# Input projection of a decoder trunk: 512 moving columns for the matmuls, halves added on eviction, the key norm moved, the convolution's taps regrouped

## The chip, the cores and the metric

One core of a Trainium2 chip runs the kernel. The metric is the device time of one execution in microseconds (us); the kernel before was run three times, with a median of 1014.74 us (1014.39 to 1015.14).

## What is computed

One decoder layer on a sequence of 256 tokens with 2048 channels, in float32. The input is normalised, projected once, and the columns of the projection are divided among three token mixers:

```python
x = layer_norm(x, ln_in_g, ln_in_b)
h = jnp.einsum("bsd,dc->bsc", x, w_in[l])                 # 2048 -> 2368 columns
c_q, c_kv, k_rope = h[..., :o1], h[..., o1:o2], h[..., o2:o3]
u_conv, u_pool = h[..., o3:o4], h[..., o4:]
y_mla  = mla_mixer(c_q, c_kv, k_rope, ...)                # 8 heads, latent q (512) and kv (256), rotary key
y_conv = conformer_conv_mixer(u_conv, ...)                # a*sigmoid(g), causal convolution of 31 taps, LN, silu
y_pool = pool_mixer(u_pool, ...)                          # trailing mean over 2/4/8/16 minus token, linear
x = layer_norm(ALPHA * x + concat(y_mla, y_conv, y_pool) @ w_out[l], ln1_g, ln1_b)
# then w_up, a convolution of 3 taps, silu gate, w_down, and a third layer norm
```

## The kernel before, in words

Channels lie on partitions, tokens along the free side, so one activation tile is 128 x 256. Every large product is made of three: weights and activations are each split into a rounded high part and the rest (`hi`, `lo` for weights; `xh`, `xl`, called x in the profile, for activations), and high*high, high*low and low*high are added in one PSUM bank. For each channel tile kt the normalised input holds `xh` and `xl` beside each other, so that both can be read as one operand of 512 columns (`X.wide(kt)`).

Weights come in units of 128 x 2048 from HBM (SP's DMA queue, two pieces of 128 x 1024). For each piece ACT rounds `hi<-raw` (line 198) and DVE subtracts `lo<-raw,hi` (line 214). `take()` hands the next unit to TensorE and stages a later one, so these two operations stand in the instruction streams several units ahead of their use.

The input projection takes its units in this order: four pairs for the convolution (value and gate of 128 channels each), a pair for the latent kv (`kvb`), one unit for the rotary key (`kr`, line 614), two pairs for the latent q, two pairs for the pooling mixer. The first convolution pair is done while the input is normalised. All other pairs go through `proj`: for each of 16 channel tiles and 2 column blocks three matmuls of 256 columns, 48 for a unit. The FFN and the kr unit already use 512 moving columns, in `proj_wide` and a loop of its own.

Between the matmuls the program puts DVE work on a queue `bgq`: for each of the four convolution tiles `acc` a first tap (`tap0`, line 573) and 30 more (line 576, `acc<-hp,pc,acc`). `bg(n)` takes n of them out, behind every unit; the table NBG holds n for convolution units, kv, kr and q units, pooling units, ukv and uq units, and units of w_out. What is left is taken out before the convolution's layer norm.

Behind the projection follow, on TensorE: the keys of 8 heads (KN, from `ckh`, `ckl`), the values V, two units of the queries (QR with the rotary part, QN), the rotations (`rope`, a matmul, and three DVE operations a tile, lines 627 to 629), the pooling mixer's linear map (line 759), and the scores of the first two heads. These read KN and QN in a first matmul and the rotated key KA and the rotated query qn[0] in a second, which must wait until DVE has finished `rope` of the first tile.

The pooling mixer (`pool_group`) copies a projected tile to `up` (ACT, line 682), forms the trailing sums on POOL by doubling (`ws`, line 687: one, two, three, four additions for the four windows), and subtracts on DVE (`dd`, line 690). Each engine runs its instructions in the order of the program.

Of the kernel before, what the change touches and what calls it, by code (L numbers as in the profile page):

```python
# [12 lines left out]
AF = mybir.ActivationFunctionType  # L13
ALU = mybir.AluOpType

P = 128
S = 256
NTB = S // P
D = 2048
KT = D // P  # L20
# [6 lines left out]
NCONV = 31  # L27
# [8 lines left out]
LASTG = 3 + NTAIL  # L36
BY_PE = 2
WARM0 = 44
NBG = (4, 4, 4, 4, 4)
RES_AT = (4, 5, 8, 11)  # L40


# [40 lines left out]
def build(tc, ctx, a, out):  # L83
    nc = tc.nc
    act, dve, pool, pe, sp = nc.scalar, nc.vector, nc.gpsimd, nc.tensor, nc.sync
    sub, mul, add = ALU.subtract, ALU.mult, ALU.add
# [54 lines left out]
    def PC(name, i=0):  # L141
        return pc[:, _PC[name] + i:_PC[name] + i + 1]

    ident = C("ident", 0, 128)
# [89 lines left out]
    def take():  # L234
        while len(staged) < LOOK + 1 and nxt[0] < len(units):
            stage_one(homes[nxt[0] - len(units)] if nxt[0] >= len(units) - NTAIL else None)
        return staged.popleft()
# [3 lines left out]
    def bg(n):  # L241
        while n > 0 and bgq:
            bgq.popleft()()
            n -= 1
# [10 lines left out]
    def mm(o, l, r, start, stop):  # L255
        pe.matmul(o, l, r, start=start, stop=stop)  # L256
# [86 lines left out]
    def m(name="m", dt=F32, w=S):  # L343
        return mp.tile([P, 288], dt, tag="m", name=nm(name), bufs=28)[:, 0:w]
# [4 lines left out]
    def pbg(n):  # L349
        while n > 0 and pq:  # L350
            pq.popleft()()
            n -= 1
# [88 lines left out]
    X = Channels("x")  # L441
# [65 lines left out]
    xh, xl = [X.hi(k) for k in range(KT)], [X.lo(k) for k in range(KT)]  # L507
# [3 lines left out]
    res_in = residual_ops(dve, a["ln_in_g"], a["ln_in_b"])  # L511


    def proj(nun, kper, ncb, ah, al, banks, nbg=0, total=None):
        total = total or nun * kper
        for u in range(nun):
            w = take()
            for k in range(kper):
                kt = u * kper + k
                s0, s1 = kt == 0, kt == total - 1  # L520
                for cb in range(ncb):
                    c = (k * ncb + cb) * P
                    o = banks[cb][:, 0:S]
                    mm(o, w(0, c, P), ah[kt], s0, False)
                    mm(o, w(0, c, P), al[kt], False, False)
                    mm(o, w(1, c, P), ah[kt], False, s1)
            bg(nbg)
            pbg(6)

    def proj_wide(x, xh, banks, nbg=0, u0=0):  # L530


        def high(w, kt, last):
            for cb in range(2):
                mm(banks[cb], w(0, ((kt % 8) * 2 + cb) * P, P), x[kt], kt == 0, last)

        def low(w, kt):
            for cb in range(2):
                mm(banks[cb][:, 0:S], w(1, ((kt % 8) * 2 + cb) * P, P), xh[kt], False, False)

        for u in range(u0, 2):
            w = take()
            kts = range(u * 8, u * 8 + 8)
            if u == 0:
                for kt in kts:
                    high(w, kt, False)
            for kt in kts:
                low(w, kt)
            if u == 1:
                for kt in kts:  # L550
                    high(w, kt, kt == KT - 1)
            bg(nbg)

    def split_ps(ps, scale, hi, lo):
        act.activation(hi, ps, AF.Identity, scale=scale)
        dve.scalar_tensor_tensor(lo, ps, scale, hi.bitcast(F32), op0=mul, op1=sub)


    accs = []
    for j in range(4):  # L560
        ba, bg_ = first if j == 0 else (bank(), bank())
        if j:
            proj(2, 8, 2, xh, xl, [ba, bg_], nbg=NBG[0])
        hp = m("hp", w=288)
        pool.memset(hp[:, 0:NCONV - 1], 0.0)
        sig = m("sig")
        act.activation(sig, bg_[:, 0:S], AF.Sigmoid)
        dve.tensor_tensor(hp[:, NCONV - 1:NCONV - 1 + S], ba[:, 0:S], sig, op=mul)
        acc = m("acc")
        accs.append(acc)  # L570

        def tap0(j=j, hp=hp, acc=acc):
            dve.tensor_scalar(acc, hp[:, 0:S], PC("conv_w", j * NCONV), PC("conv_b", j), op0=mul, op1=add)

        def tapk(k, j=j, hp=hp, acc=acc):
            dve.scalar_tensor_tensor(acc, hp[:, k:k + S], PC("conv_w", j * NCONV + k), acc, op0=mul, op1=add)  # L576
        bgq.append(tap0)
        for k in range(1, NCONV):
            bgq.append(lambda k=k, f=tapk: f(k))


    def token_rms(sqs, n):
        b = bank()
        for t in range(NTB):
            for i, q in enumerate(sqs):
                pe.matmul(b[:, t * 2:t * 2 + 2], q[:, t * P:(t + 1) * P], ones[:, 0:2], start=i == 0, stop=i == len(sqs) - 1)  # L586
        ss = small(name="ss")
        act.copy(ss[:, 0:2], b[:, 0:4:2])
        rs = small(name="rs")
        rsqrt(rs[:, 0:2], ss[:, 0:2], 2, RMS_EPS, 1.0 / n)  # L590
        return rs


    kvb = [bank(), bank()]
    proj(2, 8, 2, xh, xl, kvb, nbg=NBG[1])
    kvg, sqs = [], []
    for i in range(2):
        v = m("kvg")
        act.activation(v, kvb[i][:, 0:S], AF.Identity, scale=PC("kv_g", i))
        q = m("sq")  # L600
        act.activation(q, kvb[i][:, 0:S], AF.Square)
        kvg.append(v)
        sqs.append(q)

# [2 lines left out]
    w = take()  # L607
# [6 lines left out]
    dve.tensor_tensor(kr, krb[:, 0:S], kr, op=add)  # L614
    cs_ = cos_sin()

    rs_kv = token_rms(sqs, 256)
    diag = m("diag", w=S)
    for t in range(NTB):
        dve.tensor_scalar(diag[:, t * P:(t + 1) * P], ident, rs_kv[:, t:t + 1], None, op0=mul)  # L620

    def rope(src, cos, sin):

# [13 lines left out]
    qh, ql, qsq = [], [], []  # L637
    for c in range(2):
        qb = [bank(), bank()]
        proj(2, 8, 2, xh, xl, qb, nbg=NBG[1])  # L640
        if c == 0:
            COS, SIN = spread(cs_)

            b, b2_ = bank(), bank()
            pe.matmul(b[:, 0:S], both[:, 0:P], kr, start=True, stop=True)
            pe.matmul(b2_[:, 0:S], both[:, P:2 * P], kr, start=True, stop=True)
            t0_, t1_ = m("t0"), m("t1")
            dve.tensor_tensor(t1_, b2_[:, 0:S], SIN, op=mul)
            dve.tensor_tensor(t0_, b[:, 0:S], COS, op=mul)
            dve.tensor_tensor(KA[0:64], t0_[0:64], t1_[0:64], op=add)  # L650
            dve.tensor_tensor(KB[64:128], t0_[64:128], t1_[64:128], op=add)
            rb = bank()
            pe.matmul(rb[:, 0:S], ones, diag, start=True, stop=True)
            ch, cl = [], []
            for i in range(2):
                dve.tensor_tensor(kvg[i], rb[:, 0:S], kvg[i], op=mul)
                hh, ll = m("ckh", F32R), m("ckl", F32R)
                act.copy(hh, kvg[i])
                dve.tensor_tensor(ll, kvg[i], hh.bitcast(F32), op=sub)
                ch.append(hh)  # L660
                cl.append(ll)
        for i in range(2):
            hh, ll = m("cqh", F32R), m("cql", F32R)
            split_ps(qb[i][:, 0:S], PC("q_g", c * 2 + i), hh, ll)
            q = m("sq")
            act.activation(q, qb[i][:, 0:S], AF.Square)
            qh.append(hh)
            ql.append(ll)
            qsq.append(q)
# [7 lines left out]
    def pool_group(gi, b):  # L677
        W = WINDOWS[gi]
        PAD = 16
        up = m("up", w=288)  # L680
        pool.memset(up[:, 0:PAD], 0.0)
        act.copy(up[:, PAD:PAD + S], b[:, 0:S])
        cur, wdt = up, 1
        while wdt < W:
            n2 = m("ws", w=288)
            s_ = PAD - (W - wdt * 2)
            pool.tensor_tensor(n2[:, s_:PAD + S], cur[:, s_:PAD + S], cur[:, s_ - wdt:PAD + S - wdt], op=add)
            cur, wdt = n2, wdt * 2
        dd = m("dd")
        dve.scalar_tensor_tensor(dd, cur[:, PAD:PAD + S], 1.0 / W, up[:, PAD:PAD + S], op0=mul, op1=sub)  # L690
        fx = m("fx", w=16)
        pool.tensor_tensor(fx, cur[:, PAD:PAD + 16], C("icnt", gi * 16, 16), op=mul)
        pool.tensor_tensor(dd[:, 0:16], fx, up[:, PAD:PAD + 16], op=sub)
        return dd

    dds = []
    for c in range(2):
        pb = [bank(), bank()]
        proj(2, 8, 2, xh, xl, pb, nbg=NBG[2])
        if c == 0:  # L700
            rs_q = token_rms(qsq, 512)
            pool.tensor_scalar(rs_q[:, 2:4], rs_q[:, 0:2], SM_SCALE, None, op0=mul)
        for i in range(2):
            dds.append(pool_group(c * 2 + i, pb[i]))
# [3 lines left out]
    w = take()  # L708
    for h in range(H):
        b = bank()  # L710
        for k in range(2):
            c = k * 1024 + h * P
            o = b[:, 0:S]
# [8 lines left out]
    w = take()  # L722
    for t in range(NTB):
        ts_ = slice(t * P, (t + 1) * P)
        for n in range(2):
            b = bank()
# [30 lines left out]
    for gi in range(4):  # L757
        b = bank()
# [422 lines left out]
```

## Time and profile before

| | before |
|---|---|
| median of three runs | 1014.74 us |
| profiled execution | 1014.69 us, of which the span from the first to the last instruction is 1012.9 |
| TensorE (PE) busy | 1001.6 us, 99% |
| VectorE (DVE) busy | 703.0 us, 69% |
| ScalarE (ACT) busy | 509.6 us, 50% |
| GpSimd (POOL) busy | 53.6 us, 5% |
| mean granted TensorE clock | 0.999 of full speed |

The shares are averages over the whole span. DVE has 69% in the mean, but over the first 14 of the 40 equal slices of the span (25.3 us each) its tenths read 5 9 9 8 6 8 9 8 9 7 6 9 9 9, and later 6, 5 and 4. So its idle time is looked for stage by stage. A row of the timeline gives the start, the busy time, the engine, the line, the operation, output and inputs, shapes, and the count of consecutive instructions; in brackets the idle time before and what ended it. Since an engine takes the next instruction a little before the last has ended, the cost of an operation is read from start to start.

### The profile page before, as it was taken

The numbers are of one execution on the slowest core, as the hardware profiler recorded it, in microseconds if no ns is written. First come the engines' busy times: TensorE is split into PE (matmuls) and PEld (weight loads), VectorE is DVE, ScalarE is ACT, GpSimd is POOL, SyncE is SP. The second block draws the span as 40 slices with busy tenths as digits, with TensorE's granted clock in tenths as the row PEclk, the third lists the DMA queues.
The fourth block names the chain that finished last, engine by engine and source line by source line (L and its number), as shares of the span: only waits on it lengthen the run. The fifth ranks groups of instructions, "written<-read, shape, count | busy, mean of one in ns | idle before, by whom it ended". The sixth has DMA issues, their size and how long they took to land.

```text
span 1012.9 us, 14979 instructions
## 1 busy us (share of the span) xinstructions
PE 1001.6 (99%) x5752; PEld 883.9 (87%) x5752; DVE 703.0 (69%) x1070; ACT 509.6 (50%) x751; POOL 53.6 (5%) x95
## 2 busy tenths in 40 slices
PE   9999999999999999999999999999999999999997
PEld 8999999878898888888888888888888888888885
DVE  5998689897699966666666656666665544544566
ACT  5545466553566554555455455545544444443440
POOL 0830230000000000000000000000000000000000
PEclk9999999999999999999999999999999999999999
DMA  8655544566268655555556555655556766556542
GB/s 320 221 187 197 168 144 145 176 207 209 78 189 282 219 199 189 191 185 191 193 181 194 190 197 179 196 189 187 189 189 195 265 202 198 188 196 192 191 138 84
DMA packets 55656, 193.16 MB, mean 191 GB/s; under 512 B 6432, under 2 KB 6688, under 8 KB 55328
## 3 DMA queue, kind: packets, MB, share of 16 engines
q1 hardware_dynamic: 55152, 191.86, 56.9%
q8 instruction: 45, 0.74, 0.3%
q10 hardware_dynamic: 432, 0.35, 0.1%
q14 instruction: 27, 0.22, 0.1%
HBM read 190.08 MB, written 2.10 MB: 190 GB/s over the span
## 4 chain that ended last, share of the span: by engine, by line
PE 97%; DVE 1%; DMA 0%; ACT 0%; POOL 0%; issue 0%; POOLq 0%; SPq 0%
PE ps L256 94%; PE ps L471 1%; DMA x<-in_x 0%; PE ps L461 0%; POOL mv L263 0%; PE ps L283 0%; PE ps L586 0%; DVE lo L214 0%; DVE st L449 0%; PE ps L625 0%; PE ps L759 0%; DVE st L857 0%; DVE x L856 0%; PE ps L1058 0%; ACT hi L198 0%
## 5 line engine op out<-in xcount | busy, mean ns | idle before, releaser
L214 DVE TENSOR_TENSOR lo<-raw,hi 128x1024 fp32r<-128x1024 f32 x340 | 408.8, 1213 | 263.8 <-ACT hi L198 244.6
L198 ACT CAST hi<-raw 128x1024 fp32r<-128x1024 f32 (+1 forms) x342 | 355.1, 1044 | 396.1 <-PE ps L256 369.4
L256 PE MATMUL ps<-x,hi 128*128 128x512 f32 (+1 forms) x1984 | 425.0, 357 | 0.4 <-DVE x L293 0.4
L256 PEld LDWEIGHTS ps<-x,hi 128*128 128x128 f32 x1984 | 347.2, 189 | 52.0 <-DVE x L293 0.6
L256 PE MATMUL ps<-x,lo 128*128 128x256 f32 x1664 | 248.3, 283 | 0.0
L256 PEld LDWEIGHTS ps<-x,lo 128*128 128x128 f32 x1664 | 223.7, 192 | 3.3
L256 PE MATMUL ps<-hi,al 128*128 128x512 f32 x352 | 136.9, 389 | 0.0
L256 PE MATMUL ps<-hi,ah 128*128 128x512 f32 x352 | 136.9, 389 | 0.0
L256 PE MATMUL ps<-lo,ah 128*128 128x512 f32 x352 | 136.9, 389 | 0.0
L256 PE MATMUL ps<-hi,mx 128*128 128x512 f32 x256 | 80.5, 392 | 0.0
L256 PEld LDWEIGHTS ps<-lo,ah 128*128 128x128 f32 x352 | 66.1, 188 | 13.8
L256 PEld LDWEIGHTS ps<-hi,al 128*128 128x128 f32 x352 | 66.1, 188 | 13.7
L256 PEld LDWEIGHTS ps<-hi,ah 128*128 128x128 f32 x352 | 66.1, 188 | 13.5
L576 DVE SCALAR_TENSOR_TENSOR acc<-hp,pc,acc 128x256 f32<-128x256 f32 x120 | 59.1, 493 | 2.7
L256 PEld LDWEIGHTS ps<-hi,mx 128*128 128x128 f32 x256 | 48.1, 188 | 9.9
L263 POOL TENSOR_TENSOR mv<-mv,cc 128x1 f32<-128x1 f32 x8 | 6.8, 855 | 875.2 <-DVE mv L262 875.2
L256 PE MATMUL ps<-lo,mx 128*128 128x512 f32 x128 | 49.8, 389 | 0.0
L965 ACT COPY u<-ps 128x256 f32<-128x256 f32 x88 | 28.6, 377 | 21.8 <-PE ps L256 21.8
L966 DVE TENSOR_TENSOR u<-ps,u 128x256 f32<-128x256 f32 x88 | 33.1, 418 | 1.5 <-ACT u L965 1.5
L256 PEld LDWEIGHTS ps<-lo,mx 128*128 128x128 f32 x128 | 24.1, 188 | 4.8
L967 ACT ACTIVATE ta<-u,pc 128x256 f32<-128x256 f32 x44 | 24.2, 602 | 2.2 <-DVE u L966 2.2
L967 ACT ACTIVATE tg<-u,pc 128x256 f32<-128x256 f32 x44 | 24.2, 600 | 1.6 <-DVE u L966 1.6
(179 smaller groups left out, 634.6 us busy)
## 6 DMA issues: line engine op xcount, KB each, us to landing
raw<-in_w_up SPq DMA_DIRECT2D x174, 512.0 KB, 4.1
raw<-in_w_down SPq DMA_DIRECT2D x88, 512.0 KB, 4.1
raw<-in_w_in SPq DMA_DIRECT2D x34, 512.0 KB, 4.2
raw<-in_w_out SPq DMA_DIRECT2D x32, 512.0 KB, 4.2
raw<-in_w_uq SPq DMA_DIRECT2D x6, 512.0 KB, 3.8
x<-in_x SPq DMA_DIRECT2D x8, 256.0 KB, 5.4
plain<-in_w_in SPq DMA_DIRECT2D x4, 512.0 KB, 7.1
raw<-in_w_ukv SPq DMA_DIRECT2D x4, 512.0 KB, 4.3
```

The source lines that it names most:

```text
L198: i_ = act.copy(hi, raw[:, o:o + wd])
L214: i_ = dve.tensor_tensor(lo, raw[:, o:o + wd], w.parts[0][len(w.parts[1])].bitcast(F32), op=sub)
L256: pe.matmul(o, l, r, start=start, stop=stop)
L263: pool.tensor_tensor(mv[:, 2:3], mv[:, 1:2], nhalf[:, 0:1], op=ALU.pow)
L471: pin(pe.matmul(first[cb][:, t * P:(t + 1) * P], plain[kt // 8](((kt % 8) * 2 + cb) * P, P), vx[c][:, j, t * P:(t + 1) * P], start=kt == 0 ...
L576: dve.scalar_tensor_tensor(acc, hp[:, k:k + S], PC("conv_w", j * NCONV + k), acc, op0=mul, op1=add)
L965: act.copy(u, ps[:, S:2 * S])
L966: dve.tensor_tensor(u, ps[:, 0:S], u, op=add)
L967: act.activation(t_, u, AF.Identity, scale=PC("ffn_w", 2 * 2 * NF + blk), bias=PC("ffn_b", blk))
```

## The change

`proj` is gone. All pairs now use `proj_wide`: a weight tile of the high part meets `xh` and `xl` in one matmul of 512 columns, which leaves two halves in the bank, and the low part meets `xh` in one of 256. In the first unit of a pair all 16 high matmuls come first and then the 16 low ones, in the second unit the low ones come first. The two halves of a bank are added when it is read: `halves` copies the second half to SBUF on ACT and adds it to the first on DVE. That is done for both tiles of each of the eight pairs, and takes the place of the ACT copy in `pool_group`. The sums of squares and the reciprocal root of the kv norm (`token_rms`, `diag`) move from behind the kr unit to between the two units of the first q pair. NBG goes from 4 everywhere to 4, 6, 6, 4, 3.

```diff
-NBG = (4, 4, 4, 4, 4)
+NBG = (4, 6, 6, 4, 3)
...
-    def proj(nun, kper, ncb, ah, al, banks, nbg=0, total=None):
...
-                    mm(o, w(0, c, P), ah[kt], s0, False)
-                    mm(o, w(0, c, P), al[kt], False, False)
-                    mm(o, w(1, c, P), ah[kt], False, s1)
-            bg(nbg)
-            pbg(6)
-
-    def proj_wide(x, xh, banks, nbg=0, u0=0):
+    def proj_wide(x, xh, banks, nbg=0, u0=0, npq=0, between=None):
...
             bg(nbg)
+            pbg(npq)
+            if u == 0 and between is not None:
+                between()
...
+    def halves(b, dst=None):
+
+        t_ = m("half")
+        act.copy(t_, b[:, S:2 * S])
+        dst = t_ if dst is None else dst
+        dve.tensor_tensor(dst, b[:, 0:S], t_, op=add)
+        return dst
...
-            proj(2, 8, 2, xh, xl, [ba, bg_], nbg=NBG[0])
+            proj_wide(xw, xh, [ba, bg_], nbg=NBG[0], npq=6)
...
-        act.activation(sig, bg_[:, 0:S], AF.Sigmoid)
-        dve.tensor_tensor(hp[:, NCONV - 1:NCONV - 1 + S], ba[:, 0:S], sig, op=mul)
+        gate, val = (halves(bg_), halves(ba)) if j else (bg_[:, 0:S], ba[:, 0:S])
+        act.activation(sig, gate, AF.Sigmoid)
+        dve.tensor_tensor(hp[:, NCONV - 1:NCONV - 1 + S], val, sig, op=mul)
...
-    rs_kv = token_rms(sqs, 256)
     diag = m("diag", w=S)
-    for t in range(NTB):
-        dve.tensor_scalar(diag[:, t * P:(t + 1) * P], ident, rs_kv[:, t:t + 1], None, op0=mul)
+
+    def kv_diag():
+        rs_kv = token_rms(sqs, 256)
+        for t in range(NTB):
+            dve.tensor_scalar(diag[:, t * P:(t + 1) * P], ident, rs_kv[:, t:t + 1], None, op0=mul)
...
-        proj(2, 8, 2, xh, xl, qb, nbg=NBG[1])
+        proj_wide(xw, xh, qb, nbg=NBG[1], npq=6, between=kv_diag if c == 0 else None)
...
-            split_ps(qb[i][:, 0:S], PC("q_g", c * 2 + i), hh, ll)
+            qs_ = halves(qb[i])
+            split_ps(qs_, PC("q_g", c * 2 + i), hh, ll)
...
-        act.copy(up[:, PAD:PAD + S], b[:, 0:S])
+        halves(b, up[:, PAD:PAD + S])
...
-        proj(2, 8, 2, xh, xl, pb, nbg=NBG[2])
+        proj_wide(xw, xh, pb, nbg=NBG[2], npq=6)
```

On DVE, in the stretch of the pooling mixer, the instructions of the kernel before stand in this order (`lo` is the low part of a weight piece, `dd` the pooling difference, `acc` a convolution tap):

```order
L214 TENSOR_TENSOR lo_1545<-raw_1537,hi_1543 128x1024
L690 SCALAR_TENSOR_TENSOR dd_1528<-ws_1526,up_1521 128x256
L573 TENSOR_SCALAR acc_694<-hp_689,pc 128x256
L576 SCALAR_TENSOR_TENSOR acc_694<-hp_689,pc,acc_694 128x256 x3
L214 TENSOR_TENSOR lo_1605<-raw_1599,hi_1603 128x1024
...
L576 SCALAR_TENSOR_TENSOR acc_694<-hp_689,pc,acc_694 128x256 x4
L690 SCALAR_TENSOR_TENSOR dd_1672<-ws_1670,up_1663 128x256
L214 TENSOR_TENSOR lo_1703<-raw_1695,hi_1701 128x1024
L576 SCALAR_TENSOR_TENSOR acc_694<-hp_689,pc,acc_694 128x256
L690 SCALAR_TENSOR_TENSOR dd_1688<-ws_1686,up_1677 128x256
L576 SCALAR_TENSOR_TENSOR acc_694<-hp_689,pc,acc_694 128x256 x7
```

After the change the same engine has, in the second pair of the pooling mixer, these rows (`up` is the sum of two halves):

```order
L552 TENSOR_TENSOR up_1469<-ps_1367,half_1471 128x256
L574 SCALAR_TENSOR_TENSOR acc_642<-hp_631,pc,acc_642 128x256
L214 TENSOR_TENSOR lo_1513<-raw_1505,hi_1511 128x1024
L692 SCALAR_TENSOR_TENSOR dd_1480<-ws_1478,up_1469 128x256
L574 SCALAR_TENSOR_TENSOR acc_642<-hp_631,pc,acc_642 128x256
L552 TENSOR_TENSOR up_1485<-ps_1368,half_1487 128x256
L574 SCALAR_TENSOR_TENSOR acc_642<-hp_631,pc,acc_642 128x256 x2
L692 SCALAR_TENSOR_TENSOR dd_1498<-ws_1496,up_1485 128x256
L571 TENSOR_SCALAR acc_764<-hp_753,pc 128x256
```

`up`, which ACT wrote before, is now written by DVE itself, and between an `up` and its `dd` stand two taps, or a tap and a `lo`. The third accumulator (acc_642) ends here, where before it (acc_694) had just begun, and the fourth (acc_764) starts.

Ahead of the rotation of the queries (`t`, `qn`) the kernel before has on DVE:

```order
L576 SCALAR_TENSOR_TENSOR acc_694<-hp_689,pc,acc_694 128x256
L214 TENSOR_TENSOR lo_1913<-raw_1907,hi_1911 128x1024
L214 TENSOR_TENSOR lo_1917<-raw_1909,hi_1915 128x1024
L214 TENSOR_TENSOR lo_2065<-raw_2059,hi_2063 128x1024
L627 TENSOR_TENSOR t_320_1985<-ps_1983,cs_1186 128x256
L628 TENSOR_TENSOR qn_1856<-qn_1856,cs_1184 128x256
```

and the changed kernel:

```order
L574 SCALAR_TENSOR_TENSOR acc_764<-hp_753,pc,acc_764 128x256 x6
L214 TENSOR_TENSOR lo_1723<-raw_1717,hi_1721 128x1024
L214 TENSOR_TENSOR lo_1727<-raw_1719,hi_1725 128x1024
L574 SCALAR_TENSOR_TENSOR acc_764<-hp_753,pc,acc_764 128x256 x7
L214 TENSOR_TENSOR lo_1875<-raw_1869,hi_1873 128x1024
L628 TENSOR_TENSOR t_336_1795<-ps_1793,cs_1060 128x256
L629 TENSOR_TENSOR qn_1666<-qn_1666,cs_1058 128x256
```

Counted over the whole stream, 200 DVE instructions stand ahead of this place before and 239 after; the same number of `lo` is among them, and 16 additions of halves, 22 taps of line 574 and one first tap are new.

On TensorE the first unit of a pair begins before and after as follows (bank 399 and 400 are the two column blocks):

```order
L256 MATMUL ps_399<-x_330,hi_276 128x256 x2
L256 MATMUL ps_399<-x_330,lo_336 128x256
L256 MATMUL ps_400<-x_330,hi_276 128x256 x2
L256 MATMUL ps_400<-x_330,lo_336 128x256
L256 MATMUL ps_399<-x_330,hi_276 128x256 x2
```

```order
L256 MATMUL ps_399<-x_330,hi_276 128x512
L256 MATMUL ps_400<-x_330,hi_276 128x512
L256 MATMUL ps_399<-x_330,hi_276 128x512
L256 MATMUL ps_400<-x_330,hi_276 128x512
L256 MATMUL ps_399<-x_333,hi_276 128x512
```

Two matmuls of 256 columns on one weight tile have become one of 512; the low ones follow behind the 16 high ones.

## Rows read from the trace of the kernel before

**Rows 1.** The page's busy times: engine, us, share of the span, instructions.

```profile
PE 1001.6 (99%) x5752; PEld 883.9 (87%) x5752; DVE 703.0 (69%) x1070; ACT 509.6 (50%) x751; POOL 53.6 (5%) x95
```

**Rows 2.** The page's chain that ended last, by engine.

```profile
PE 97%; DVE 1%; DMA 0%; ACT 0%; POOL 0%; issue 0%; POOLq 0%; SPq 0%
```

**Rows 3.** Timeline of TensorE: the first of eight projection units, and what follows them.

```profile
27.55 0.48 PE L256 MATMUL ps<-x,hi 128*128 128x256 f32 x2
...
73.70 3.82 PE L256 MATMUL ps<-x,hi 128*128 128x512 f32 x16
```

**Rows 4.** Timeline of TensorE in the FFN, where the wide helper runs.

```profile
300.31 4.00 PE L256 MATMUL ps<-x,lo 128*128 128x256 f32 x32
304.14 7.44 PE L256 MATMUL ps<-x,hi 128*128 128x512 f32 x32
311.42 0.76 PE L256 MATMUL ps<-x,lo 128*128 128x256 f32 x5
```

**Rows 5.** Groups of DVE from 97.3 to 137.1 us: busy, mean ns, idle before.

```profile
L214 DVE TENSOR_TENSOR lo<-raw,hi 128x1024 fp32r<-128x1024 f32 x12 | 14.7, 1224 | 5.9 <-ACT hi L198 5.5 <-PE ps L256 0.5
L576 DVE SCALAR_TENSOR_TENSOR acc<-hp,pc,acc 128x256 f32<-128x256 f32 x16 | 8.6, 535 | 0.4
L690 DVE SCALAR_TENSOR_TENSOR dd<-ws,up 128x256 f32<-128x256 f32 x4 | 2.1, 535 | 6.4 <-POOL ws L687 6.4
L556 DVE SCALAR_TENSOR_TENSOR cql<-ps,pc,cqh 128x256 fp32r<-128x256 f32 x4 | 1.9, 481 | 1.4 <-ACT cqh L555 1.4
```

**Rows 6.** Timeline of DVE in the projection: weight pieces and taps.

```profile
74.39 1.22 DVE L214 TENSOR_TENSOR lo<-raw,hi 128x1024 fp32r<-128x1024 f32 x1
75.52 3.08 DVE L576 SCALAR_TENSOR_TENSOR acc<-hp,pc,acc 128x256 f32<-128x256 f32 x6
78.52 2.35 DVE L214 TENSOR_TENSOR lo<-raw,hi 128x1024 fp32r<-128x1024 f32 x2
```

**Rows 7.** Timeline of DVE up to the rotation of the queries.

```profile
148.54 0.48 DVE L576 SCALAR_TENSOR_TENSOR acc<-hp,pc,acc 128x256 f32<-128x256 f32 x1
148.94 3.68 DVE L214 TENSOR_TENSOR lo<-raw,hi 128x1024 fp32r<-128x1024 f32 x3
152.54 0.42 DVE L627 TENSOR_TENSOR t<-ps,cs 128x256 f32<-128x256 f32 x1
152.88 0.42 DVE L628 TENSOR_TENSOR qn<-qn,cs 128x256 f32<-128x256 f32 x1
```

**Rows 8.** Timeline of TensorE at the first scores.

```profile
154.40 0.38 PE L256 MATMUL ps<-kn,qn 128*128 128x128 f32 x2
154.62 0.39 PE L256 MATMUL ps<-KA,qn 128*128 128x128 f32 x2
```

**Rows 9.** Timeline of POOL in the pooling mixer.

```profile
116.58 1.08 POOL L693 TENSOR_TENSOR dd<-fx,up 128x16 f32<-128x16 f32 x1
...
119.83 0.61 POOL L687 TENSOR_TENSOR ws<-ws 128x256 f32<-128x256 f32 x1
...
121.06 0.24 POOL L693 TENSOR_TENSOR dd<-fx,up 128x16 f32<-128x16 f32 x1
...
134.35 2.36 POOL L687 TENSOR_TENSOR ws<-ws 128x268 f32<-128x268 f32 x3
```

**Rows 10.** Timeline of DVE beside those instructions of POOL.

```profile
116.33 1.24 DVE L214 TENSOR_TENSOR lo<-raw,hi 128x1024 fp32r<-128x1024 f32 x1
...
129.51 2.88 DVE L576 SCALAR_TENSOR_TENSOR acc<-hp,pc,acc 128x256 f32<-128x256 f32 x4
```

**Rows 11.** Windows near the end: length, busy of PE, PEld, DVE, ACT, POOL, then granted clock, DMA.

```profile
1003.80:1006.40 2.60, 0.03 (x1) 0.00 (x0) 2.53 (x6) 0.39 (x2) 0.92 (x1) 1.00 0.00 0
1008.40:1009.50 1.10, 0.05 (x1) 0.00 (x0) 0.61 (x1) 0.59 (x1) 0.00 (x0) 1.00 0.65 248
...
1011.50:1012.00 0.50, 0.00 (x0) 0.00 (x0) 0.00 (x0) 0.00 (x0) 0.00 (x0) 0.50 0.00 0
```

**Rows 12.** Timeline of TensorE: the matmuls on zeros that open the kernel.

```profile
1.10 7.02 PE L253 MATMUL ps<-wz 128*128 128x256 f32 x44 [1.10 <-POOL hp L565]
```

More of the change, by code (lines that the diff above doesn't have):

```diff
@@ L511, in build @@
     res_in = residual_ops(dve, a["ln_in_g"], a["ln_in_b"])
-    def proj(nun, kper, ncb, ah, al, banks, nbg=0, total=None):
[L515 to L523, printed above, removed]
-                    mm(o, w(0, c, P), ah[kt], s0, False)
-                    mm(o, w(0, c, P), al[kt], False, False)
-                    mm(o, w(1, c, P), ah[kt], False, s1)
-            bg(nbg)
-            pbg(6)
-    def proj_wide(x, xh, banks, nbg=0, u0=0):
+    def proj_wide(x, xh, banks, nbg=0, u0=0, npq=0, between=None):
         def high(w, kt, last):
@@ L556, in split_ps @@
         dve.scalar_tensor_tensor(lo, ps, scale, hi.bitcast(F32), op0=mul, op1=sub)
+    xw = [X.wide(k) for k in range(KT)]
+    def halves(b, dst=None):
[4 more added lines that the diff above has]
+        return dst
     accs = []
@@ L594, in build @@
     kvb = [bank(), bank()]
-    proj(2, 8, 2, xh, xl, kvb, nbg=NBG[1])
+    proj_wide(xw, xh, kvb, nbg=NBG[1], npq=6)
     kvg, sqs = [], []
     for i in range(2):
+        kv = halves(kvb[i])
         v = m("kvg")
-        act.activation(v, kvb[i][:, 0:S], AF.Identity, scale=PC("kv_g", i))
+        act.activation(v, kv, AF.Identity, scale=PC("kv_g", i))
         q = m("sq")
-        act.activation(q, kvb[i][:, 0:S], AF.Square)
+        act.activation(q, kv, AF.Square)
         kvg.append(v)
@@ L663, in build @@
             hh, ll = m("cqh", F32R), m("cql", F32R)
-            split_ps(qb[i][:, 0:S], PC("q_g", c * 2 + i), hh, ll)
+            qs_ = halves(qb[i])
+            split_ps(qs_, PC("q_g", c * 2 + i), hh, ll)
             q = m("sq")
-            act.activation(q, qb[i][:, 0:S], AF.Square)
+            act.activation(q, qs_, AF.Square)
             qh.append(hh)
```

## The prediction

> **What bounds the kernel now.** I read the page's busy times first: PE has 1001.6 us of the 1012.9-us span [rows 1], and the chain that ended last lies on PE for 97% [rows 2]. So what shortens PE shortens the kernel, as long as the engines behind it keep up. DVE, which does the new work, has 69% in the mean, and a mean says nothing of the stage that is changed. I therefore read DVE's timeline through the projection. Up to 97 us it stands back to back, a piece of `lo` every 1.13 us and a tap every half microsecond [rows 6]. Its idle time is between 97.3 and 137.1 us [rows 5], where it waits for ACT's `hi` (5.5 us, which in turn waits for PE to free a buffer), for POOL's sums (6.4) and for ACT's `cqh` (1.4). Then it is busy again until it starts the rotation of the queries at 152.54 [rows 7]. PE needs the rotated tile at 154.62 [rows 8]; the tile is ready four operations of 0.34 us after 152.54, at about 153.9. That margin of 0.7 us is the place that decides: everything that DVE is given ahead of it must fit into the idle 14 us, or PE stands still there.
>
> **PE's gain.** Eight units took 73.70 - 27.55 = 46.15 us [rows 3], 5.77 each. The FFN runs the same wide form: 32 matmuls of 256 columns in 304.14 - 300.31 = 3.83 us, 0.120 each, and 32 of 512 in 311.42 - 304.14 = 7.28, 0.2275 each [rows 4]. A unit becomes 16 × 0.2275 + 16 × 0.120 = 5.56, which is 0.205 less. Sixteen units give 3.3 us. PE then comes to the first scores at 154.40 - 3.3 = 151.1. The columns that pass are the same; only the starts are fewer. The order of high and low in a unit costs nothing: the first `lo` of a second unit is needed about when DVE has it. Moving the kv norm costs nothing either: its sums are wanted by PE 4 us after the squares are there, where before they stood right behind kr; without that cover it would be some tenths.
>
> **DVE's new work ahead of the rotation.** Thirty-nine instructions are added and no `lo` is removed. Sixteen halves: each is an operation of 128x256 with one input in PSUM, as `t` is, 152.88 - 152.54 = 0.34 [rows 7], together 5.3. The 22 taps cost 0.50 in a row of six (78.52 - 75.52 = 3.00) [rows 6] and 0.40 alone (148.94 - 148.54) [rows 7], since in a row each waits for the one before; that is 0.40 + 0.12 for each neighbour. With 0.12 × 22 the taps are 11.4 and the first tap 0.45. The 16 halves and `up`s stand between taps and break rows of them, which saves about 17 × 0.12 = 2.0. Sum 5.3 + 11.4 + 0.45 - 2.0 = 15.1 us.
>
> **What it fits into.** The 39.8 us from 97.3 to 137.1 hold 12 `lo`, 16 taps, 4 `dd` and 4 `cql` [rows 5] and a first tap. At 1.135, 0.45, 0.35, 0.39 and 0.45 (start to start) these are 13.6 + 7.2 + 1.4 + 1.6 + 0.45 = 24.2 us, so 15.6 are to be had, if nothing is waited for; with two shorter gaps next to it some 16.5. All waits for `hi` and `cqh` go: DVE is 3 us later there and PE, which frees ACT, is earlier. Without waits DVE would be at the rotation at 152.5 + 15.1 - 16.5 = 151.1, just when PE arrives.
>
> **The waits that do not go.** POOL's sums are now formed from an `up` that DVE itself has just written, so they cannot run ahead of a late DVE. Between an `up` and its `dd` DVE has only two taps (0.9 us) or a tap and a `lo` (1.5). One addition on POOL takes 0.61 to 0.70 [rows 9], in a row 2.36 / 3 = 0.79. And POOL does not get on beside a `lo`: its small `dd` took 1.08 beside the `lo` that ran from 116.33 to 117.5 [rows 9, 10], and 0.24 at 121.06 with no `lo` beside it [rows 9]. So, from the end of an `up` and with 0.2 for the two hand-overs:
> - window 2: 0.6 + 1.1 (frozen by the `lo`) + 0.2 = 1.9, cover 1.5, wait 0.4;
> - window 4: 2 × 0.7 + 0.2 = 1.6, cover 0.9, wait 0.7;
> - window 8: 3 × 0.7 + 1.1 + 0.2 = 3.4, cover 1.5, wait 1.8;
> - window 16: 4 × 0.79 + 0.2 = 3.4, cover 0.9, wait 2.5.
>
> Together 5.4 us. From below it is 4.0 (0.61 for an addition, the `lo` not blocking in the first); from above 7.4, if taps block POOL as well: beside POOL four taps took 2.88 instead of some 2.0 [rows 10]. I take 5.4, nearer to the rows at which DVE waits and disturbs nobody.
>
> On this the Trainium skill (SBUF — State Buffer, Who interferes with whom) says that a DVE instruction with two SBUF inputs and a POOL instruction that reads SBUF exclude each other for a whole instruction, and that issue order decides who waits. The trace agrees for the `lo` (1.08 against 0.24). By the rule the taps would shut POOL out as well, which is the upper bound above, 2 us later than my sum.
>
> **Sum.** DVE starts the rotation at 151.1 + 5.4 = 156.5, and the first tile is ready 1.3 later, at 157.8, 3.2 us after 154.62; row by row I get 157.7, which I take. So PE loses its 3.3 us and 3.1 more: 1014.7 + 3.1 = 1017.8. The scores' bank, which is that of the first `t`, comes free at 156.8, so PE stands still from 151.1 for 5.7 us, and nearly 1 us again for the tile. Behind it everything on PE is as before, and DVE has 23 operations fewer to do, so nothing is handed back later; the conv norm's short wait stays.
>
> **The clock in that gap.** Near the end PE ran nothing for 2.6 us and the granted clock stayed at 1.00; after its last matmul, at 1008.45, it was at 0.50 in the window from 1011.5 [rows 11]. That is from 2.4 to 1.2 GHz after an idle time shorter than the 5.7 us here. What a return costs no row shows directly. From below it is nothing, if the clock does not fall. As the other bound I take the opening matmuls: 44 took 7.02 us [rows 12] instead of 44 × 0.12 = 5.3, a loss of 1.7. I take 1.7, since the gap is nearly twice the one that left the clock alone. That makes 1014.69 + 3.1 + 1.7 = 1019.5, against the profiled execution; the median of the runs, 1014.74, stands at the same place.
>
> The Trainium skill (TensorE: Matmul & The Clock Gate, Why this matters for your kernels) warns that idle gaps between bursts of matmuls in mid-kernel bring the clock back to the lower level. The trace agrees at its end; no row of this case shows it in the middle.
>
> **Rivals.**
> 1. *PE's gain is kept.* If the halves and taps find more room than I count, DVE reaches the rotation by 150 us. The time is 1014.7 - 3.3 = 1011.4, or up to 1012.7 with a remainder of the wait. For it speaks that DVE is idle in a third of the stretch before; against it that POOL's four chains end in DVE waits whatever the room. It decides at 5 us less on DVE than I sum, so the waits for POOL would have to vanish.
> 2. *DVE late, clock kept.* 1017.8, or 1016.5 with waits at their lower bound. For it: the 2.6-us gap in which the clock stayed.
> 3. *DVE late by little.* Rotation at 153 to 155, time within 2 us of before, and no gap long enough for the clock: 1013 to 1016.7.
> 4. *A bank is missing first.* `up` also frees a PSUM bank that the keys and V need; DVE's `up` of windows 8 and 16 would be at about 129.5 and 134, PE wants the banks at 129.5 and 135. If DVE is 2 us later still (the upper bound above), PE stops there too, but that time is taken off the later gap, so the sum is 1020 to 1021 with the clock.
>
> **How the numbers follow.** The likeliest case, late with a fallen clock, has 0.42 together with rival 4 (1018 to 1021); rival 2 has 0.21, rival 3 0.18, rival 1 0.19. A measurement of this kernel can tell about 0.2%, 2.0 us, from no change, so faster is below 1012.7 and slower above 1016.8. Faster: 0.19. Same: rival 3 and the low end of rival 2, 0.21. Slower: 0.60. The range from 1012.2 to 1020.8 leaves out most of rival 1 and the last of rival 4. The likeliest case's own range is 1018.2 to 1020.8.
>
> **What would show it.** PE's units at 5.56 us and the start of kr moved from 73.70 to about 72.2; DVE without waits for `hi` from 97 to 137, but with four waits of `dd` for `ws` of 0.4 to 2.5 us; `t` starting near 156.5; one wait of PE of over 4 us for DVE's `t` ahead of the first scores, and a short one for qn; granted clock 0.50 in a window behind it, matmuls there at twice 0.12. It is wrong if PE's wait there is under 1 us, or if `dd` finds its sums ready.

## The result and the profile after

The changed kernel took 1021.27 us (median of four, 1020.93 to 1021.87) against 1014.66 of the kernel before: ratio 1.0064, 95% interval 1.0052 to 1.0076, 6.6 us slower. The forecast was slower as well, 1019.5, with a range up to 1020.8, which the time passes by 0.5 us. Its profiled execution took 1021.40 us with a span of 1019.5. The page's first part, to be read beside [rows 1]:

```profile
PE 1003.4 (98%) x5496; PEld 872.9 (86%) x5496; DVE 706.9 (69%) x1086; ACT 512.5 (50%) x763; POOL 58.2 (6%) x95
```

TensorE has 256 matmuls less and is busy longer. Where it stands is shown by its waits over the whole span (line, what it waited for, us in total, times, longest):

```profile
PE ps L256 <- DVE t L628: 5.7, 1, 5.7
PE ps L1060 <- ACT dr L1057: 2.6, 1, 2.6
...
PE ps L256 <- DVE qn L630: 0.2, 1, 0.2
```

The first and the last line are new. The timeline of TensorE at the first scores, beside [rows 8]:

```profile
149.70 1.89 PE L761 MATMUL ps<-dd,wp 128*128 128x256 f32 x8
157.25 0.80 PE L256 MATMUL ps<-kn,qn 128*128 128x128 f32 x2 [5.66 <-DVE t L628]
158.25 0.80 PE L256 MATMUL ps<-KA,qn 128*128 128x128 f32 x2 [0.20 <-DVE qn L630]
...
162.49 0.47 PE L256 MATMUL ps<-cqh,hi 128*128 128x256 f32 x1
```

The same two places before, the pooling mixer's product and the first matmul behind the scores:

```profile
152.67 1.89 PE L759 MATMUL ps<-dd,wp 128*128 128x256 f32 x8
...
156.83 0.47 PE L256 MATMUL ps<-cqh,hi 128*128 128x256 f32 x1
```

TensorE is at the scores 3 us earlier than before and leaves them 5.7 us later. DVE's timeline just ahead of it, beside [rows 7], shows what it waited for, seven taps and a weight piece in front of the rotation:

```profile
152.13 3.60 DVE L574 SCALAR_TENSOR_TENSOR acc<-hp,pc,acc 128x256 f32<-128x256 f32 x7
155.65 1.22 DVE L214 TENSOR_TENSOR lo<-raw,hi 128x1024 fp32r<-128x1024 f32 x1
156.78 0.42 DVE L628 TENSOR_TENSOR t<-ps,cs 128x256 f32<-128x256 f32 x1
```

And the windows of TensorE there (length, busy time and matmuls, granted clock, DMA) show the second part of the loss:

```profile
152.00:154.00 2.00, 0.00 (x0) 1.00 0.89 270
154.00:156.00 2.00, 0.00 (x0) 0.85 0.63 246
156.00:158.00 2.00, 0.75 (x2) 0.50 0.14 31
158.00:160.00 2.00, 1.80 (x6) 0.50 0.69 252
160.00:162.00 2.00, 2.00 (x8) 0.50 0.00 0
162.00:164.00 2.00, 2.00 (x16) 0.95 0.00 0
```

In the gap the granted clock goes to 0.50, that is 1.2 GHz, and it is back near 1.00 only in the window from 162 us, some 5 us after the engine went back to work. From the first KA to the next unit TensorE takes 162.49 - 158.25 = 4.24 us, where before it took 156.83 - 154.62 = 2.21.

There is a third part that nothing in the change touches. At the end of the kernel TensorE waits 2.63 us for ACT, before and after; before, the granted clock stayed at 1.00 through it [rows 11]. The same windows after:

```profile
1011.50:1012.00 0.50, 0.00 (x0) 0.00 (x0) 0.50 (x2) 0.43 (x2) 0.04 (x1) 1.00 0.00 0
1012.00:1012.50 0.50, 0.48 (x1) 0.42 (x2) 0.50 (x2) 0.47 (x2) 0.00 (x0) 0.64 0.00 0
1012.50:1013.00 0.50, 0.50 (x2) 0.04 (x1) 0.50 (x1) 0.09 (x1) 0.00 (x0) 0.50 0.00 0
```

The last matmuls run at the low clock; from the last small product, two matmuls ahead of that wait, to the end of the span it is 1019.5 - 1008.37 = 11.1 us, before 1012.9 - 1002.81 = 10.1.

```profile
1002.81 1.02 PE L1049 MATMUL ps<-b,cc 128*128 128x512 f32 x2
```

```profile
1008.37 1.02 PE L1051 MATMUL ps<-b,cc 128*128 128x512 f32 x2
```

Added up on the profiled executions, from the first projection matmul on (27.33 after, 27.55 before): the first KA is 130.92 us behind it instead of 127.07, so 3.85 lost; the scores lose 2.03; up to the end of the last large product 0.1 comes back; the end loses 1.0. The sum is 6.8, less 0.2 for the earlier start: the 6.6 us by which the spans differ.

### The profile page after: what moved, and what is told of

It reads as the page before. It is cut to its first block, busy times and chain, and to the rows that moved or that the text cites. A ratio compares the mean times of both kernels' runs of the same rounds, so it can differ in the third digit from the quotient of the medians.

```text
span 1019.5 us, 14502 instructions
## 1 busy us (share of the span) xinstructions
PE 1003.4 (98%) x5496; PEld 872.9 (86%) x5496; DVE 706.9 (69%) x1086; ACT 512.5 (50%) x763; POOL 58.2 (6%) x95
## 4 chain that ended last, share of the span: by engine, by line
PE 96%; DVE 2%; DMA 1%; ACT 0%; issue 0%; POOL 0%; SPq 0%; POOLq 0%; DVEq 0%
PE ps L256 92%; PE ps L471 1%; DVE lo L214 1%; DVE acc L574 1%; DMA x<-in_x 0%; DMA raw<-in_w_out 0%; PE ps L461 0%; PE ps L283 0%; PE ps L584 0%; POOL mv L263 0%; PE ps L1060 0%; PE ps L1061 0%; DVE st L859 0%; DVE x L858 0%; SPq L117 0%
## 5 line engine op out<-in xcount | busy, mean ns | idle before, releaser
L256 PE MATMUL ps<-x,hi 128*128 128x512 f32 (+1 forms) x1728 | 392.7, 384 | 0.4 <-DVE x L293 0.4
L256 PEld LDWEIGHTS ps<-x,hi 128*128 128x128 f32 x1728 | 314.8, 188 | 61.4 <-DVE x L293 0.6
L256 PEld LDWEIGHTS ps<-x,lo 128*128 128x128 f32 x1664 | 206.6, 192 | 4.3 <-DVE lo L214 0.4
L256 PE MATMUL ps<-x,lo 128*128 128x256 f32 x1664 | 208.5, 283 | 0.0
```

## The experiments

Since the start of the projection itself moves from one execution to the next (27.0 to 30.6 us over the profiles, with the wait of the transposes for x), the places below are counted from the first projection matmul of each profile. Each ratio is against runs of the kernel before made beside that kernel. Two columns stand for what decides the rotation: where DVE starts the last `dd`, and how many taps it runs between that and the rotation.

| kernel | ratio to before, 95% | last `dd` | taps behind it | rotation (t) starts | first KA | last small product |
|---|---|---|---|---|---|---|
| before | | 109.20 | 15 | 124.99 | 127.07 | 975.26 |
| after | 1.0064, 1.0052 to 1.0076 | 110.00 | 23 | 129.45 | 130.92 | 981.04 |
| taps 4, 4, 4, 4, 4 in after | 1.0001, 0.9992 to 1.0011 | 107.77 | 18 | 124.69 | 126.16 | 975.04 |
| taps 4, 6, 6, 4, 3 in before | 1.0077, 1.0062 to 1.0092 | 108.35 | 26 | 129.48 | 130.95 | 981.18 |
| POOL adds the halves | 1.0079, 1.0064 to 1.0094 | 111.58 | 23 | 131.15 | 132.62 | 983.15 |
| filled gap | 1.0083, 1.0066 to 1.0101 | 110.00 | 23 | 129.45 | 130.92 | 982.61 |
| taps 4, 6, 6, 0, 4 in after | 0.9984, 0.9971 to 0.9997 | 110.02 | 0 | 122.26 | 124.33 | 972.83 |
| taps 4, 6, 6, 0, 4 in before | 0.9998, 0.9986 to 1.0011 | 109.54 | 0 | 125.10 | 127.20 | 975.44 |
| norm behind kr (with 4, 6, 6, 0, 4) | 1.0029, 1.0017 to 1.0041 | 112.60 | 0 | 126.66 | 128.73 | 977.25 |
| taps 4, 4, 0, 0, 12 in after | 1.0096, 1.0074 to 1.0117 | 105.97 | 0 | 122.15 | 124.23 | 984.15 |
| pooling pairs narrow | 1.0093, 1.0065 to 1.0120 | 110.51 | 28 | 131.42 | 132.89 | 983.41 |

**The taps alone undone.**

```diff
-NBG = (4, 6, 6, 4, 3)
+NBG = (4, 4, 4, 4, 4)
```

> The changed kernel with the taps grouped 4, 4, 4, 4, 4 as before: wide matmuls, halves and the moved key norm stay, 23 taps go back behind the queries' rotation. Theory (DVE is late at the rotation because of the taps put ahead of it on top of the halves): DVE has 11 us less ahead, TensorE's 5.7-us wait for t disappears, the clock stays at 1.00 and the gain of 3.3 us shows: about 1011.4, at most 1013. Rival (the halves and the waits for POOL alone make DVE late): a wait of over 2 us for t stays, 1016 or more.

Measured: 1015.45 us, no difference from before. The long wait and the fallen clock at the scores are gone, as the theory said, but the gain is missing too, and the time lies above the theory's 1013: TensorE, 2.8 us earlier, still waits for DVE (t 0.98, qn 0.51, p 0.49), because DVE starts the rotation no earlier than in the kernel before (124.69, 124.99). So the taps are the loss, but the rotation's time is not the sum of DVE's work up to it: 23 taps, some 11 us by the sum, came out of that work, and the rotation is 4.8 us earlier; 16 halves more than in the kernel before, and it is where it was.

**The taps alone done.** In the kernel before:

```diff
-NBG = (4, 4, 4, 4, 4)
+NBG = (4, 6, 6, 4, 3)
```

> The kernel before with only the taps grouped 4, 6, 6, 4, 3. Theory: the added 11 us of taps fit into the 14 us in which DVE is idle there, because ACT still writes up and POOL's sums do not wait for DVE; the rotation starts at 152.5 to 153.5 and TensorE waits under 1 us: 1014.7 to 1015.7. Rival (the taps alone make DVE late): a wait of several us ahead of the first scores, 1017 or more.

Measured: 1022.5 us, and the rival is right. With narrow matmuls, no halves and ACT's `up`, the rotation starts at the same place as in the changed kernel, 129.48, and the KA and the end of the last product are as late. The regrouping of the taps is enough for the whole loss. That the place agrees to 0.03 us is partly luck: here the last `dd` comes 1.65 us earlier than in the changed kernel, and 26 taps follow it instead of 23. Its wait of TensorE was only 2.8 us, and still the granted clock fell behind it:

```profile
PE ps L256 <- DVE t L627: 2.8, 1, 2.8
```

```profile
159.00:160.00 1.00, 0.49 (x2) 1.00 0.00 0
160.00:161.00 1.00, 0.52 (x2) 0.60 0.79 274
161.00:162.00 1.00, 1.00 (x5) 0.50 0.63 250
```

**The waits for POOL.** In the changed kernel, POOL adds what ACT has copied:

```diff
-        halves(b, up[:, PAD:PAD + S])
+        h0, h1 = m("half"), m("half")
+        act.copy(h0, b[:, 0:S])
+        act.copy(h1, b[:, S:2 * S])
+        pool.tensor_tensor(up[:, PAD:PAD + S], h0, h1, op=add)
```

> The changed kernel, but the pooling mixer's two halves are copied by ACT and added by POOL, so that up does not pass through DVE. Theory (5 us of DVE's lateness are waits for sums that start from an up DVE has just written): the four waits of dd become under 1.5 us together, DVE is some 5 to 6 us earlier, the rotation starts at 150.5 to 152 and TensorE waits under 1.5 us, clock at 1.00: 1011.4 to 1013. Rival (POOL, which has four additions more and is shut out beside DVE's pieces, is just as late): dd waits 4 us or more and the time stays above 1018.

Measured: 1022.87 us; the rival is right. The `dd` waited 5.8 us in two waits, and the rotation was 1.7 us later. POOL's queue shows why:

```profile
129.35 0.11 POOL L683 MEMSET up<- 128x16 f32 x1
134.56 0.33 POOL L698 TENSOR_TENSOR dd<-fx,up 128x16 f32<-128x16 f32 x1 [5.10 <-DVE dd L695]
134.85 0.74 POOL L687 TENSOR_TENSOR up<-half,half 128x256 f32<-128x256 f32 x1
```

The first 16 columns of a `dd` are mended by POOL after DVE has written it, and the next window's sums stand behind that on POOL. So POOL waits for a DVE that is late, and then DVE waits for POOL. In the changed kernel itself POOL waits, within the windows, for DVE's `up`, as the prediction had it; the third window:

```profile
129.67 1.87 POOL L689 TENSOR_TENSOR ws<-up 128x262 f32<-128x262 f32 x1 [7.09 <-DVE up L552]
```

With `up` taken from DVE, the wait for the `dd` to be mended takes its place here. To see whether `up` matters at all, the two pooling pairs went back to the narrow form of before:

```diff
-        proj_wide(xw, xh, pb, nbg=NBG[2], npq=6)
+        proj_narrow(xw, xh, xl, pb, nbg=NBG[2])       # the old proj, three matmuls of 256
...
-        halves(b, up[:, PAD:PAD + S])
+        act.copy(up[:, PAD:PAD + S], b[:, 0:S])
```

> The changed kernel, but the two pooling pairs are multiplied in 256 columns as before, so that ACT alone writes up; the six other pairs stay wide, the taps 4, 6, 6, 4, 3. Theory of the prediction (the four waits of dd, 5 us, come from an up that DVE itself writes late): the waits fall below 2 us, DVE is 3 to 5 us earlier at the rotation, counted from the first projection matmul, and TensorE, 0.8 us slower, waits 1 to 2 us: 1015 to 1017. Rival (POOL's chain is slow by itself and dd waits for it in every version, as with ACT's up in the kernel before; what makes DVE late is what stands behind the last dd): waits of dd of 4 us or more, rotation within 1 us of the changed kernel, wait for t of 4 us, fallen clock: 1020 to 1022.

Measured: 1026.24 us, above the ranges of both. The `dd` waited 4.8 us, and the rotation is 2 us later than in the changed kernel, not earlier; the rival had allowed 1. POOL waits for DVE's `dd` here too:

```profile
131.98 0.80 POOL L703 TENSOR_TENSOR ws<-up 128x270 f32<-128x270 f32 x1
136.58 1.14 POOL L709 TENSOR_TENSOR dd<-fx,up 128x16 f32<-128x16 f32 x1 [3.79 <-DVE dd L706]
137.68 2.15 POOL L703 TENSOR_TENSOR ws<-ws 128x268 f32<-128x268 f32 x3
```

So the waits of `dd` do not go, whoever writes `up`. In the kernels so far the last `dd` is 107.8 to 111.6 us behind the projection's start, and DVE, which runs in order, cannot take work across it. Behind it stand seven `lo` (six here) and the taps of the table, and DVE runs these without a wait: the rotation follows 15.8 us behind the last `dd` with 15 taps, 16.9 with 18, 19.5 with 23 and 21.1 with 26. What stands behind the last `dd` sets the rotation. The 2 us of this kernel are that too: 28 taps and one `lo` less, behind a `dd` 0.5 us later.

**Nothing behind the last dd.** In the changed kernel:

```diff
-NBG = (4, 6, 6, 4, 3)
+NBG = (4, 6, 6, 0, 4)
```

The order on DVE up to the last `dd` is that of the changed kernel; behind it stand seven `lo` and then the rotation, and no tap.

> The changed kernel with the taps grouped 4, 6, 6, 0, 4: 93 taps instead of 116 ahead of the rotation, and none between the last dd and the rotation (the 23 of the changed kernel that stood there go behind it). Theory (the 23 taps between the last dd and the rotation make DVE late, and the grouping 4, 4, 4, 4, 4 gained nothing because it puts as many there): DVE is ready before TensorE, no wait for t, clock at 1.00, and the 3.3 us of the wide matmuls show: 1011.4, or up to 1012.5 with later waits. Rival (something else in the projection takes the gain, so that 1015 is what the wide form gives): 1014 to 1015.5.

Measured: 1015.23 us, against 1015.48 of the runs of before beside it: 0.9984 (0.9971 to 0.9997), from 1012.05 upwards where before begins at 1014.40. DVE's timeline shows that it now waits for TensorE instead (`hi` is freed by it):

```profile
137.28 0.43 DVE L692 SCALAR_TENSOR_TENSOR dd<-ws,up 128x256 f32<-128x256 f32 x1 [2.04 <-POOL ws L689]
137.62 4.67 DVE L214 TENSOR_TENSOR lo<-raw,hi 128x1024 fp32r<-128x1024 f32 x4
142.72 2.45 DVE L214 TENSOR_TENSOR lo<-raw,hi 128x1024 fp32r<-128x1024 f32 x2 [0.43 <-ACT hi L198]
148.37 1.23 DVE L214 TENSOR_TENSOR lo<-raw,hi 128x1024 fp32r<-128x1024 f32 x1 [3.20 <-ACT hi L198]
149.52 0.42 DVE L628 TENSOR_TENSOR t<-ps,cs 128x256 f32<-128x256 f32 x1
```

In the changed kernel the same instruction:

```profile
137.33 0.43 DVE L692 SCALAR_TENSOR_TENSOR dd<-ws,up 128x256 f32<-128x256 f32 x1 [2.05 <-POOL ws L689]
```

The last `dd` is at the same place, and the rotation 7.3 us earlier. TensorE does not wait, and up to the last small product the profile is 2.43 us ahead of before, most of the 2.8 that TensorE gains. In the time less comes through, and it lies in the rival's range: by the ratio 1.6 us, with an interval from 0.3 to 2.9, and only 0.25 between the medians. The 2.63-us wait near the end let the clock fall in this profile as well, and the start moves from run to run by more than the gain. That start explains the medians, as far as a grouping made afterwards can: the twelve times stand in two groups, five up to 1013.75 and seven from 1015.18, those of before in two as well, 17 up to 1015.88 and 12 from 1016.46. The medians of the lower groups are 1012.95 and 1015.02, of the upper 1015.64 and 1017.8, so group against group some 2 us come through.

As a control, the same line in the kernel before:

```diff
-NBG = (4, 4, 4, 4, 4)
+NBG = (4, 6, 6, 0, 4)
```

> The kernel before with the taps grouped 4, 6, 6, 0, 4: as many taps ahead of the rotation (93), but none between the last dd and it. Theory (TensorE bounds the kernel before at that place, DVE has 0.7 us to spare): no change, 1014.7. Rival (the place of the taps alone gains, and the wide form has nothing to do with it): 1012 or less.

Measured: 1016.73 us, ratio 0.9998; the rotation starts at 125.10, no earlier. The theory holds: there TensorE is the bound, and the room gives nothing.

**The key norm not moved.** As the kernel with 4, 6, 6, 0, 4, with `kv_diag()` called behind the kr unit:

```diff
+    kv_diag()
...
-        proj_wide(xw, xh, qb, nbg=NBG[1], npq=6, between=kv_diag if c == 0 else None)
+        proj_wide(xw, xh, qb, nbg=NBG[1], npq=6, between=None)
```

> The kernel of the first run of this batch with the kv norm's sums back behind the kr unit. Theory (the squares now pass through ACT, DVE and ACT, so the sums there are late): TensorE waits 2 to 3 us for the square, about 1013.5 to 1014.5. Rival (squares are there in time, the move does nothing): as the first run of this batch.

Measured: 1019.14 us. The theory is right about the wait and too low on its cost: 4.4 us more up to the first KA, of which 2.3 are the waits in this timeline of TensorE, and 2.1 the clock, which reads 0.53 and 0.50 from 83 to 86 us.

```profile
80.19 0.38 PE L584 MATMUL ps<-cc,sq 128*128 128x2 f32 x2 [1.14 <-ACT sq L600]
80.43 0.48 PE L256 MATMUL ps<-x,hi 128*128 128x512 f32 x1
82.11 0.83 PE L584 MATMUL ps<-cc,sq 128*128 128x2 f32 x6 [1.19 <-ACT sq L600]
82.80 5.25 PE L256 MATMUL ps<-x,hi 128*128 128x512 f32 x15
```

The last row holds most of that price: fifteen matmuls of 512 columns, 15 × 0.2275 = 3.4 us at the full clock, took 5.1 from the first start to the start of what follows.

**Still fewer taps early.** The changed kernel with 62 taps ahead of the rotation:

```diff
-NBG = (4, 6, 6, 4, 3)
+NBG = (4, 4, 0, 0, 12)
```

> The changed kernel with the taps grouped 4, 4, 0, 0, 12: only 62 taps ahead of the rotation. Theory (once DVE is ahead of TensorE at the rotation, fewer taps give nothing more, and the other 62 fit into the waits of the output projection): no wait for t, 1011.4 to 1012.5. Rival (the taps that are left collide with the attention's softmax or the convolution's norm): a wait for p or yn of more than 1 us, 1013 or more.

Measured: 1026.46 us. The rotation is no earlier than with 93 taps (122.15, 122.26), as the theory said, but the taps that are left stand in front of the convolution's norm, as the rival said, and the clock fell across these waits:

```profile
PE ps L833 <- DVE mv L262: 4.1, 1, 4.1
...
PE ps L820 <- DVE acc L574: 2.2, 1, 2.2
```

**The gap filled.** The changed kernel with work for TensorE in the wait:

```diff
         b = bank()
+        if gi == 3:
+            for _ in range(44):
+                mm(b[:, 0:S], qh[0][:, 0:P], qh[0], True, True)
         pe.matmul(b[:, 0:S], wp[:, gi * P:(gi + 1) * P], dds[gi], start=True, stop=True)
```

> The changed kernel with 44 matmuls of 256 columns on data at hand, 5.3 us, in front of the pooling mixer's last matmul, where TensorE would wait for t anyway; they are overwritten. Theory (the wait let the clock fall, which cost about 2 us more behind it): the first score still starts near 157.3, the granted clock stays at 1.00, and 2.0 us come back: about 1019.2, or 1018.2 if the fall near the end goes too. Rival (the slow scores are not the clock's doing): no change, 1021.3.

Measured: 1023.84 us; neither. The clock stayed at 1.00 and the scores took 2.31 us again (161.47 to 163.78), so the slow scores are the clock's doing:

```profile
161.47 0.49 PE L256 MATMUL ps<-KA,qn 128*128 128x128 f32 x2 [0.51 <-DVE qn L630]
...
163.78 0.47 PE L256 MATMUL ps<-cqh,hi 128*128 128x256 f32 x1
```

But the order of DVE behind the rotation changed as well (the order of most instructions is chosen when the program is built, and here weight pieces and taps came between the `mx` and the softmax), and TensorE then waited twice for `p`:

```profile
172.51 0.33 PE L798 MATMUL ps<-cc,p 128*128 128x128 f32 x1 [1.41 <-DVE p L792]
```

The last small product is 1.6 us later than in the changed kernel, so the 2 us were lost again behind the scores, and 1.6 more; the two waits are 2.8 of these 3.5. What the gap would cost with a held clock and an unchanged order was not tried.

## Why the forecast fell short

**TensorE's gain.** Forecast 3.3 us, measured 2.75 from the first projection matmul to the pooling mixer's product (149.70 - 27.33 = 122.37 after, 152.67 - 27.55 = 125.12 before). The pace of the wide form holds: 16 matmuls of 512 in 31.08 - 27.33 = 3.75 us. The rest is 0.5 us at the low parts of the first two units, which were not there in time; I had said that this cost nothing.

**Where it is lost.** The place was right, and its numbers close: rotation at 156.5, measured 156.78; TensorE standing for 5.7, measured 5.66; four waits of `dd` of 0.4, 0.7, 1.8 and 2.5, together 5.4, measured 0.51, 0.51, 1.90 and 2.05. First KA 3.1 later, measured 3.6, or 3.85 from the projection's start. For the half microsecond DVE's waits have one candidate: `diag` waited 0.90 us for POOL's `rs`. The moved key norm, which I put at nothing, put its POOL part where DVE, in order, could not go round it. No run tests whether that reaches the rotation.

**The step that failed: the term for the clock.** I took one fall and 1.7 us. The fall at the scores cost 2.03, and a second one, at the 2.63-us wait near the end, which I had put at nothing, 1.0. I had read that wait in the profile of before as a gap that leaves the clock alone. One profile could not show that: in eleven profiles of this case the same wait took 2.63 us each time, and in six the clock fell soon enough to slow all four matmuls behind it, among them those of the slowest and of the fastest execution profiled; in one more it caught only the last two. Nothing in the runs shows what decides it. Nor is it shown to be the change's own: the profile of before, with a mean clock of 0.999, is one without that fall, while 24 of the 29 runs of before made beside the kernel with 4, 6, 6, 0, 4 have 0.998 or less, as two profiles have whose only fall was at the end. With 2.0, 1.0 and 0.5 in place of 1.7, 0 and 0, the sum comes to the time.

**A reason that was only half right though its sum was right.** I held that the waits of `dd` do not go because DVE writes `up` itself. In the changed kernel POOL does wait for that `up`, but the waits of `dd` are about as long when ACT or POOL writes it (5.0 in the changed kernel; 6.4 in the kernel before, 5.4 in it with the new taps, 5.8 where POOL adds the halves and 4.8 with narrow pooling pairs). In the last two of these kernels POOL waits 6.0 and 7.2 us for DVE's `dd`, so that there the two engines seem to wait for each other; in the kernel before it waits 0.4 for them, with the new taps 0.9, and `dd` waits all the same. No run took the mending of `dd` off POOL, so what sets these waits in every version stays open. What the change adds at the rotation is shown by the places: of the 4.5 us by which it is later (129.45 against 124.99), 0.8 lie ahead of the last `dd` and 3.65 behind it, where 23 taps stand instead of 15. Without any tap there the same DVE is 7.3 us earlier. And the halves, 5.3 us in my sum, cost little by themselves: with 4, 4, 4, 4, 4 the last `dd` is 1.4 us earlier than before and the rotation is where it was; the idle time of DVE ahead of the last `dd` can take most of them up. So the forecast of the rotation, 0.3 us from the measured one, owes something to luck: it put all new work into one balance of work and idle time, where the last `dd` divides it. Two slips in its working change little: window 8 leaves 3.4 - 1.5 = 1.9, not 1.8, and 5.7 us is more than twice the 2.6-us gap, not nearly.

**The rivals.** The gain was kept only in part and only without those taps. My condition for it, 5 us less on DVE, is borne out (7.3 were given, and the wait went; how little would do was not tried). I had looked for them in the waits for POOL. The bank that could have been missing was not: TensorE has no wait between the projection and the scores.

**The clock rule.** That a pause of TensorE in mid-kernel takes the clock down, which the Trainium skill (TensorE: Matmul & The Clock Gate, Why this matters for your kernels) warns of, the traces here show at 5.66 us, at 2.80, at two of 1.2 with two matmuls of 2 columns and one of 512 between, and in seven of eleven profiles at 2.63. The Trainium skill speaks there of longer gaps than the last three; here the measurement decides.

## What to carry to other kernels

An engine that is idle in the mean can be the bound of one hand-over. Find the last place ahead of it that the engine cannot pass (here the last `dd`, tied to POOL), and count only what stands between that and the hand-over; work put there costs its full length (8 taps 3.65 us), work ahead of it much less (31 taps more there, some 14 us at 0.45 each, moved the last `dd` by 4 us, from 105.97 to 110.02). Price a pause of TensorE with what it does to the clock behind it: here 2 us at the scores on top of the 5.7 waited.

## What was not expected of the hardware

The granted clock fell behind pauses that one would call short: after 2.80 us and even across two of 1.14 and 1.19, and in both it came back to 1.00 some 3 us after it fell. The same 2.63-us pause dropped it in some executions and not in others. The beginning moves too: the first projection matmul stood at 27.0 to 30.6 us in the profiles of one case, with TensorE's wait for the normalised x between nothing and 3.0 us. The profiles show why: the fourth of the eight loads of x landed at 6.3 to 7.2 us in six of them, which start the projection at 27.0 to 27.8, and at 8.1 to 8.9 in the other five, which start it at 29.3 to 30.6. So single times of this kernel differ by 3 us and more for reasons that have nothing to do with the change, and places counted from that matmul are what can be compared.
